# A convolution tap moved from GpSimd to ScalarE, and a weight split issued in quarters, in a two-layer hybrid sequence kernel

## The chip, the cores and the metric

The kernel runs on one core of a Trainium2 chip. The core has five engines that work side by side: TensorE (PE in the profile, with its weight loads as PEld), VectorE (DVE), ScalarE (ACT), GpSimd (POOL) and SyncE (SP), which here only issues DMAs. Each engine takes its instructions in a fixed order, and semaphores hold an instruction until what it needs is there. The metric is the device time of one execution in microseconds; smaller is better.

## What is computed

A trunk of two layers over 2048 frames of 1024 channels. Each layer normalises the residual stream, scales and shifts it with vectors that come from a conditioning input, mixes, and adds the gated result back. The first layer mixes with a linear recurrence, the second with a gated delta rule of 8 heads of 128 channels in chunks of 64 frames. Ahead of both stands a causal depthwise convolution of width 4. Cut to what matters here:

```python
def causal_dwconv(x, w):
    k = w.shape[0]
    xp = jnp.pad(x, ((0, 0), (k - 1, 0), (0, 0)))
    out = xp[:, 0:s] * w[0]
    for j in range(1, k):
        out = out + xp[:, j:j + s] * w[j]
    return out

def gated_deltanet_block(h, in_w, conv_w, a_log, dt_bias, onorm_g, out_w):
    proj = h @ in_w
    qkv = jax.nn.silu(causal_dwconv(proj[..., :o1], conv_w))
    z = proj[..., o1:o2]
    ...
    q = l2norm(q) * (GDN_DK ** -0.5)
    k = l2norm(k)
    ...
    o = chunk_gated_delta_rule(q, k, v, g, beta)
    o = o * lax.rsqrt(jnp.mean(o * o, axis=-1, keepdims=True) + EPS) * onorm_g
    return (o * jax.nn.silu(z)) @ out_w
```

All is float32. The large products are made from two parts of each operand, a rounded high part and a low part (what the rounding left): high by high, high by low and low by high.

## The kernel before

**Tiling and stages.** Channels lie on the 128 partitions, frames along the free axis in tiles of `TC` = 512. The frames go through each layer in two halves (`u` = 0 and 1, `T` = 1024 frames, two tiles each). In the second layer every half runs over heads; a head has a weight panel of 128 output channels for k, v and q each, and z panels are spread between the heads. A panel serves two jobs, one for each tile of 512 frames, and a job is 24 matmuls (8 pieces of the 1024 input channels by three products, L668) into one PSUM bank. After the second layer's heads comes the output projection with the final norm.

**Weight panels.** `panels_thread` loads a panel of 128x1024 as `raw`, ACT rounds it to the high part `whi` (L644), and in the first half GpSimd subtracts to get the low part `wlo` (L650), in one instruction of 1024 columns; `keep_thread` then writes `wlo` to HBM, and in the second half it is read back from there. `raw`, `whi` and `wlo` have two buffers each. So L650 runs 48 times: 16 panels of the first layer and 32 of the second, all in the halves u = 0.

**Convolution of the second layer.** `conv2_thread` takes a job's PSUM bank `pt`. `extend` puts it into `xe`, a tile of 4 + 512 columns: GpSimd copies the last four columns of the tile before (`carry`) or zeros into the first four (L724, L728), ACT copies the 512 out of PSUM (L730), the bank is free, and GpSimd saves the last four for the next tile (L733). Then GpSimd multiplies `xe`, shifted, by the first tap's weights into `xf` (L997), and DVE adds the other three taps with one instruction each (`taps`, L718). ACT's tanh (L1009) and a product on DVE (L1014) make the SiLU and with it `kt`, `vt` or `qt`; then `xf` is free. `xe` and `xf` have two buffers each. There are 96 such convolutions, 48 in each half. (In the first layer, `convolve` makes the last tap on ACT straight from PSUM, L746, and the others on DVE from PSUM, L756.)

**What stands around it.** From `kt` PE makes transposes and products (L1135, L1169), DVE inverts small 32x32 blocks of 8 chunks at a time in 62 short dependent steps (L1292, L1295), and then runs the recurrence over the chunks: products with the state (L1412, L1413), a combination on DVE (L1421), a product with the inverse (L1429), an ACT copy (L1435), two products (L1441, L1442) and the state's update on DVE (L1454). GpSimd has the inverse square roots (L243), masks (L1124), short copies, and part of the low parts of the activations (L572).

**The order.** The program writes the order of every engine's queue by itself. Class `Weave` runs threads against a model of time: before an instruction a thread yields the engine and an estimated cost in microseconds (`yield "pool", 2.3`), at times with the lag until its result is seen, or a set of buffers, or an event; the thread whose turn is earliest goes next, and a priority breaks ties. The engines then carry out their queues in that order, whatever the real durations are. A changed cost can so change the order of everything behind it.

## Time and profile before

| | |
|---|---|
| runs, median of 3 | 1934.21 us (1933.47 to 1941.75) |
| profiled execution, span | 1937.1 us |
| mean granted TensorE clock | 0.984 |
| first layer's input side | 0 to about 500 us |
| first layer's output projection | 500 to 668 |
| second layer, u = 0 | 668 to 1190 |
| second layer, u = 1 | 1190 to about 1743 |
| output projection, final norm | 1743 to 1937 |
| L650, 48 times | 2519 ns mean, 120.9 us |
| L997, 96 times | 782 ns mean, 75.1 us |
| L730, 96 times | 579 ns mean, 55.5 us |
| L718, 288 times | 784 ns mean, 224.9 us |
| L1014 (kt, vt, qt) | 32 times each |

The span is that of one profiled execution, from its first to its last instruction; the profile gives no time around it. The other times are whole executions. Rows of the profile name a line of the kernel, the engine, the operation and what is written from what; after "x" stands the count, then busy microseconds and the mean of one in ns, then the idle time of the engine before these instructions and what ended most of it. A chain row follows the work that ended last back from its end. A row of a line's own view gives minimum, median and maximum in ns. A row of stages has the stretch, its length, then the busy time and count for PE, PEld, DVE, ACT and POOL, the clock, the DMA share and GB/s.

### The profile page before, as it was taken

How to read it: one execution, taken by the hardware profiler on the slowest of the kernel's cores; microseconds unless marked ns; L12 is line 12 of the kernel's file. 1: busy time of each engine (PE TensorE's matmuls, PEld its weight loads, DVE VectorE, ACT ScalarE, POOL GpSimd, SP SyncE). 2: the span in 40 equal slices, each digit the busy share in tenths (PEclk: the TensorE clock that was granted, in tenths of full speed). 3: DMA queues.
4: the chain of work that ended last, by engine and by line, in shares of the span. 5: the costliest groups of instructions: out<-in, count | busy, mean ns of one | idle time of the engine just before them, and what ended most of it. 6: DMA issues, size and time to landing. Idle time of an engine off the chain costs nothing.

```text
span 1937.1 us, 31289 instructions
## 1 busy us (share of the span) xinstructions
PE 1844.0 (95%) x10286; PEld 1503.9 (78%) x10286; DVE 1471.2 (76%) x3175; ACT 1048.2 (54%) x2587; POOL 654.8 (34%) x1116
## 2 busy tenths in 40 slices
PE   6999999999899999898999999999999999999998
PEld 3787778878688877677787877788888888888887
DVE  6898998887544668869888896769777878886653
ACT  3666677667212345375565663565666656654321
POOL 3344542223100235345445543333332334411110
PEclk9999999999899999999999998999999999999999
DMA  8476746554578735446676565555365555687751
GB/s 320 116 219 189 223 138 220 175 167 138 169 204 236 208 106 145 128 111 160 166 186 141 138 158 150 149 156 158 102 163 143 140 140 139 155 246 207 230 161 66
DMA packets 511723, 322.77 MB, mean 167 GB/s; under 512 B 371268, under 2 KB 439236, under 8 KB 511560
## 3 DMA queue, kind: packets, MB, share of 16 engines
q1 hardware_dynamic: 511560, 320.77, 59.1%
q8 instruction: 81, 1.33, 0.3%
q14 instruction: 82, 0.67, 0.1%
HBM read 219.93 MB, written 100.73 MB: 166 GB/s over the span
## 4 chain that ended last, share of the span: by engine, by line
PE 61%; DVE 20%; DMA 6%; issue 4%; ACT 4%; SPq 3%; POOL 2%; DVEq 0%; POOLq 0%; ACTq 0%
PE mm L668 31%; PE mmo L668 16%; DVE xf L718 2%; DVE ttmp L1292 2%; DVE tblk L1295 2%; PE pg L807 1%; PE py L1429 1%; PE pp L1412 1%; PE pS L1442 1%; PE pqk L1257 1%; PE pS L1441 1%; PE pp L1413 1%; PE pkk L1169 1%; DVE xf L756 1%; DMA raw<-in_w 1%
## 5 line engine op out<-in xcount | busy, mean ns | idle before, releaser
L718 DVE SCALAR_TENSOR_TENSOR xf<-xe,cw_s,xf 128x512 f32<-128x512 f32 x288 | 224.9, 784 | 20.6 <-POOL xf L997 18.1
L650 POOL TENSOR_TENSOR wlo<-raw,whi 128x1024 fp32r<-128x1024 f32 x48 | 120.9, 2519 | 143.6 <-ACT whi L644 115.4
L1292 DVE TENSOR_TENSOR ttmp<-blk,tblk 128x60 f32<-128x60 f32 (+24 forms) x496 | 125.4, 253 | 16.6 <-DMA blk<-blk_d 5.4
L1295 DVE TENSOR_TENSOR tblk<-tblk,ttmp 128x60 f32<-128x60 f32 (+24 forms) x496 | 124.8, 252 | 10.7
L644 ACT CAST whi<-raw 128x1024 fp32r<-128x1024 f32 x96 | 100.2, 1044 | 50.3 <-DMA raw<-in_w 44.5
L668 PE MATMUL mmo<-oh,yh 128*128 128x512 f32 x256 | 102.1, 399 | 4.8 <-ACT oh L907 4.8
L668 PE MATMUL mm<-hh_('in2', 0)_5342,whi 128*128 128x512 f32 x256 | 105.3, 411 | 0.0
L668 PE MATMUL mm<-hh_('in2', 0)_5437,whi 128*128 128x512 f32 x256 | 105.3, 411 | 0.0
L668 PE MATMUL mmo<-ol,yh 128*128 128x512 f32 x256 | 102.2, 399 | 3.0 <-DVE ol L909 3.0
L668 PE MATMUL mm<-hh_('in2', 0)_5342,wlo 128*128 128x512 f32 x256 | 104.7, 409 | 0.0
L668 PE MATMUL mm<-hl_('in2', 0)_5343,whi 128*128 128x512 f32 x256 | 104.7, 409 | 0.0
L668 PE MATMUL mm<-hl_('in2', 0)_5438,whi 128*128 128x512 f32 x256 | 104.1, 407 | 0.0
L668 PE MATMUL mm<-hh_('in2', 1)_12030,wlo 128*128 128x512 f32 x256 | 104.1, 407 | 0.0
L668 PE MATMUL mm<-hl_('in2', 1)_12219,whi 128*128 128x512 f32 x256 | 104.0, 406 | 0.0
L668 PE MATMUL mm<-hh_('in2', 0)_5437,wlo 128*128 128x512 f32 x256 | 103.9, 406 | 0.0
L668 PE MATMUL mm<-hh_('in2', 1)_12218,whi 128*128 128x512 f32 x256 | 103.6, 405 | 0.0
L668 PE MATMUL mm<-hh_('in2', 1)_12030,whi 128*128 128x512 f32 x256 | 103.5, 404 | 0.0
L668 PE MATMUL mm<-hl_('in2', 1)_12031,whi 128*128 128x512 f32 x256 | 103.3, 403 | 0.0
L668 PE MATMUL mm<-hh_('in2', 1)_12218,wlo 128*128 128x512 f32 x256 | 103.2, 403 | 0.0
L668 PE MATMUL mmo<-ol,oh 128*128 128x512 f32 (+1 forms) x264 | 103.1, 391 | 0.0
L668 PE MATMUL mmo<-oh,ol 128*128 128x512 f32 (+1 forms) x264 | 103.1, 391 | 0.0
L668 PE MATMUL mmo<-oh,oh 128*128 128x512 f32 (+1 forms) x264 | 103.0, 390 | 0.0
(331 smaller groups left out, 5649.8 us busy)
## 6 DMA issues: line engine op xcount, KB each, us to landing
raw<-in_w SPq DMA_DIRECT2D x96, 512.0 KB, 4.2
araw<-in_ada_w SPq DMA_DIRECT2D x32, 512.0 KB, 4.3
xt<-x_d SPq DMA_DIRECT2D x32, 512.0 KB, 4.9
xt_d<-xb SPq DMA_DIRECT2D x192, 64.0 KB, 2.4
xk<-xt_d SPq DMA_DIRECT2D x24, 512.0 KB, 6.1
xt<-in_x SPq DMA_DIRECT2D x16, 512.0 KB, 4.4
ada<-in_ada_w SPq DMA_DIRECT2D x16, 512.0 KB, 8.5
y_d<-tz SPq DMA_DIRECT2D x32, 256.0 KB, 3.2
```

The source lines that it names most:

```text
L644: act.copy(hi, raw)
L650: pool.tensor_tensor(lo, raw, f(hi), ALU.subtract)
L668: pe.matmul(pt, lhsT=lhs[a][:, k, :], rhs=rhs[b][:, k, :], start=(k == 0 and n == 0), stop=(k == KT - 1 and n == 2))
L718: dve.scalar_tensor_tensor(xf, xe[:, 1 + j:1 + j + TC], wc[:, j:j + 1], xf, ALU.mult, ALU.add)
L756: dve.scalar_tensor_tensor(xf[:, 3:TC], pt[:, j:j + TC - 3], wc[:, j:j + 1], xf[:, 3:TC], ALU.mult, ALU.add)
L807: pe.matmul(pg, lhsT=a[:, g, :], rhs=b, start=(q == 0), stop=(q == 2))
L1169: pe.matmul(pkk[:, b, :], lhsT=kc, rhs=kc, start=True, stop=True)
L1257: pe.matmul(pqk[:, b, :], lhsT=kt[:, b * P:(b + 1) * P], rhs=qt[:, b * P:(b + 1) * P], start=True, stop=True)
L1292: dve.tensor_tensor(tmp, blk[:, j, j + 1:32].unsqueeze(2).to_broadcast([P, r, c_]), t[:, j, 0:c_].unsqueeze(1).to_broadcast([P, r, c_]), A ...
L1295: dve.tensor_tensor(t[:, j + 1:32, 0:c_], t[:, j + 1:32, 0:c_], tmp, ALU.subtract)
L1412: pe.matmul(pp[:, 0, :], lhsT=kc, rhs=S_, start=True, stop=True)
L1413: pe.matmul(pp[:, 1, :], lhsT=qc, rhs=S_, start=True, stop=True)
```

## The change

There are two edits and a clean-up. In the second layer's convolution the last tap (the one that lies on the frame itself) is made by ACT, straight from the PSUM bank, with the weights as a scale per partition, ahead of the copy to `xe`; GpSimd's multiply is gone, and DVE adds taps 0, 1 and 2 in place of 1, 2 and 3. For this `xf` is taken before the bank is read. In `panels_thread` the low part comes in four instructions of 256 columns each, with a planned cost of 0.63 in place of one of 2.3. The switch `POOLED`, which was empty, is dropped with what hung on it.

```diff
@@ panels_thread
-                    yield "pool", 2.3
-                    pool.tensor_tensor(lo, raw, f(hi), ALU.subtract)
+                    for q in range(0, KT, 2):
+                        yield "pool", 0.63, 0.2 if q == KT - 2 else 0.0
+                        sl = slice(q, q + 2)
+                        pool.tensor_tensor(lo[:, sl, :], raw[:, sl, :], f(hi[:, sl, :]), ALU.subtract)
                     put("raw", rtok)
                     w.spawn(keep_thread(p, lo), 5)
@@
-    def taps(xe, xf, wc, j0=1):
-        for j in range(j0, 4):
-            yield "dve", STT, 0.13 if j < 3 else 0.27
+    def taps(xe, xf, wc):
+        for j in range(3):
+            yield "dve", STT, 0.13 if j < 2 else 0.27
             dve.scalar_tensor_tensor(xf, xe[:, 1 + j:1 + j + TC], wc[:, j:j + 1], xf, ALU.mult, ALU.add)
 
-    def extend(xe, pt, mtok, bank, carry, key, g):
+    def extend(xe, xf, last, pt, mtok, bank, carry, key, g):
...
+        yield "act", 0.53, 0.0
+        act.activation(xf, pt, AF.Copy, scale=last)
         yield "act", CP
         act.copy(xe[:, 4:4 + TC], pt)
         put(bank, mtok)
@@ conv2_thread
-        yield from extend(xe, pt, mtok, bank, carry2[:, idx, :], (kind, h), u * NTC + i)
         ftok = yield slots["xf"]
-        yield "pool", 0.68
         xf = tile_([P, TC], "xf", "xf")
-        pool.tensor_scalar(xf, xe[:, 1:1 + TC], cw2_s[:, idx, 0:1], 0.0, ALU.mult, ALU.add)
+        yield from extend(xe, xf, cw2_s[:, idx, 3:4], pt, mtok, bank, carry2[:, idx, :], (kind, h), u * NTC + i)
         ttok = yield slots["tt"]
-        if kind in POOLED:
...
-        yield from taps(xe, xf, cw2_s[:, idx, :], 2 if kind in POOLED else 1)
+        yield from taps(xe, xf, cw2_s[:, idx, :])
```

## The prediction

> **What bounds the kernel now.** I read the page first, then the chain of waits by stage, then the groups of instructions and the waits of the two halves of the second layer (u = 0 from 668 us to 1190, u = 1 from there to 1743), and last two short pieces of the timeline.

> ```profile
> PE 1844.0 (95%) x10286; PEld 1503.9 (78%) x10286; DVE 1471.2 (76%) x3175; ACT 1048.2 (54%) x2587; POOL 654.8 (34%) x1116
> PE 61%; DVE 20%; DMA 6%; issue 4%; ACT 4%; SPq 3%; POOL 2%; DVEq 0%; POOLq 0%; ACTq 0%
> ```

> PE carries 61% of the chain that ended last, DVE 20%; GpSimd, which the change relieves, only 2%. The stages differ, though. These are the chain by line, 668 to 1190 and then 1190 to 1743, and the busy time by engine of the same two stages.

> ```profile
> by line: PE mm L668 27.3%; DVE xf L718 7.6%; DVE ttmp L1292 7.4%; DVE tblk L1295 6.3%; issue 4.9%; PE pqk L1257 2.0%; PE pab L1055 1.4%; ACT junkq L1208 1.3%; PE pkk L1169 1.3%; PE px L1363 1.3%; DVE kt L1014 1.2%; DMA pq<-q_d 1.2%; SPq L13
> ```
> ```profile
> by line: PE mm L668 54.7%; PE pp L1412 2.7%; PE py L1429 2.6%; PE pS L1442 2.4%; DMA zs<-z_d 2.4%; PE pkk L1169 2.4%; PE pp L1413 2.3%; PE pS L1441 2.3%; PE pqk L1257 1.9%; PE pr L1373 1.7%; issue 1.4%; DMA vn<-v_d 1.3%; PE px L1334 1.3%; D
> ```
> ```profile
> 668.00:1190.00 522.00, 484.68 (x3068) 398.07 (x3067) 420.68 (x1036) 293.67 (x895) 245.38 (x436) 0.98 0.57 145
> 1190.00:1743.00 553.00, 546.62 (x3600) 455.21 (x3599) 432.02 (x1222) 337.69 (x1039) 183.47 (x414) 0.99 0.57 152
> ```

> In the first half DVE's taps (L718), its two lines of the small inverses (L1292, L1295) and the product L1014 hold at least 22.5% of the chain, the projection's matmuls 27.3%: DVE and PE share the bound. In the second half the matmuls of L668 alone have 54.7%, and no DVE line is above 1.3%. A microsecond won for DVE is worth something in the first half and next to nothing in the second.

> What makes the first half so? The taps and the inverse there, then the same groups in the second half:

> ```profile
> L718 DVE SCALAR_TENSOR_TENSOR xf<-xe,cw_s,xf 128x512 f32<-128x512 f32 x144 | 116.3, 811 | 13.5 <-POOL xf L997 12.1
> L1292 DVE TENSOR_TENSOR ttmp<-blk,tblk 128x54 f32<-128x54 f32 (+24 forms) x224 | 65.3, 292 | 7.0 <-DMA tt_d<-ttmp 1.5 <-DMA blk<-blk_d 1.4
> L1295 DVE TENSOR_TENSOR tblk<-tblk,ttmp 128x54 f32<-128x54 f32 (+24 forms) x224 | 60.7, 271 | 4.8
> L650 POOL TENSOR_TENSOR wlo<-raw,whi 128x1024 fp32r<-128x1024 f32 x30 | 74.9, 2496 | 81.7 <-ACT whi L644 64.3 <-DMA wlo_d2z<-wlo 8.5 <-DMA q_d<-tb 4.2
> L997 POOL TENSOR_SCALAR xf<-xe,cw_s 128x512 f32<-128x512 f32 x48 | 37.7, 785 | 1.7 <-DMA raw<-in_w 1.5
> ```
> ```profile
> L718 DVE SCALAR_TENSOR_TENSOR xf<-xe,cw_s,xf 128x512 f32<-128x512 f32 x144 | 108.6, 757 | 7.1 <-POOL xf L997 6.0
> L1295 DVE TENSOR_TENSOR tblk<-tblk,ttmp 128x60 f32<-128x60 f32 (+24 forms) x248 | 59.0, 238 | 5.3
> L1292 DVE TENSOR_TENSOR ttmp<-blk,tblk 128x60 f32<-128x60 f32 (+24 forms) x248 | 55.0, 222 | 9.2 <-DMA blk<-blk_d 4.1
> ```

> L650 runs only in the first half, L997 equally in both (48 each). Without L650 a tap costs 757 ns, with it 811; the inverse's lines 222 and 238 against 292 and 271. The differences come to 54 ns x 144 + 70 ns x 224 + 33 ns x 224 = 31 us of DVE time beside 74.9 us of L650, 0.41 us for each. How, the timeline shows:

> ```profile
> 746.18 2.48 POOL L650 TENSOR_TENSOR wlo<-raw,whi 128x1024 fp32r<-128x1024 f32 x1 [2.79 <-ACT whi L644]
> 746.18 0.21 DVE L1292 TENSOR_TENSOR ttmp<-blk,tblk 128x52 f32<-128x52 f32 x1
> 746.42 2.30 DVE L1295 TENSOR_TENSOR tblk<-tblk,ttmp 128x52 f32<-128x52 f32 x1
> ...
> 758.78 2.39 POOL L650 TENSOR_TENSOR wlo<-raw,whi 128x1024 fp32r<-128x1024 f32 x1
> 758.86 2.86 DVE L1161 TENSOR_TENSOR ec<-ec,cc 128x512 f32<-128x512 f32 x1
> 761.11 0.66 POOL L733 COPY carry<-xe 128x4 f32<-128x4 f32 x1
> 761.75 0.69 POOL L997 TENSOR_SCALAR xf<-xe,cw_s 128x512 f32<-128x512 f32 x1
> 761.89 0.63 DVE L1295 TENSOR_TENSOR tblk<-tblk,ttmp 128x65 f32<-128x65 f32 x1
> ```

> A DVE instruction of 0.21 us takes 2.30 and ends just behind L650. Then they alternate: L1161 ends at 761.72, the carry copy waits for it (0.66 us), L997 goes, and the next step of the inverse takes 0.63. Only one of the two moves at a time.

> **The change part by part.** The prices come from these rows (all taps of the trace; ACT's PSUM copy and the carry; a copy with an immediate scale and one with a scale per partition, both 128x128 from PSUM; ACT's tap in the first layer, with scale and bias; GpSimd's subtract of a quarter's size):

> ```profile
> L718 DVE SCALAR_TENSOR_TENSOR xf<-xe,cw_s,xf x288: 702/748/2885, 676.8 to 1698.3; 128x512 f32<-128x512 f32 x144
> L730 ACT COPY xe<-mm x96: 561/582/594, 675.0 to 1691.3; 128x512 f32<-128x512 f32 x96
> L733 POOL COPY carry<-xe x96: 178/188/749, 675.8 to 1691.9; 128x4 f32<-128x4 f32 x96
> L1435 ACT ACTIVATE yt<-py x128: 253/278/291, 817.6 to 1802.9; 128x128 f32<-128x128 f32 x128
> L1468 ACT ACTIVATE t<-pp,eg x120: 346/368/373, 820.8 to 1801.8; 128x128 f32<-128x128 f32 x120
> L746 ACT ACTIVATE xf<-mm,cb_s,cw_s x32: 762/778/782, 56.3 to 473.4; 128x509 f32<-128x509 f32 x32
> L875 POOL TENSOR_TENSOR gl<-gw,gh x16: 732/1053/1502, 53.0 to 468.7; 128x256 fp32r<-128x256 f32 x16
> ```

> *ACT's new tap.* A per-partition scale adds 368 - 278 = 90 ns, so 582 + 90 = 0.67 us, between 0.58 (the copy) and 0.78 (L746). 48 a half are +32 us of ACT in each, 294 to 326 of 522 and 338 to 370 of 553. Behind it wait the xe copy, the release of the PSUM bank (0.67 us later: PE has a second bank, and with 30 panels of two jobs in 522 us a job comes every 8.7; uncovered it would be 32 us a half), then the tanh, the key's scalings, the recurrence's yt. An ACT instruction finds a tap running one time in 16 (32/522) and waits 0.34 us: 895 x 0.06 x 0.34 = 18 us of delay spread over all of them, and ACT lines hold little of the chain: +1.5 us a half (0 to 9).

> *L997 goes.* From the job's end to the first tap stood copy, carry and L997: 0.58 + 0.28 + 0.78 = 1.64 us; now tap and copy, 1.25, with no place in GpSimd's queue. DVE makes three taps either way. DVE's waits for L997 in the first half (us, times, longest):

> ```profile
> DVE xf L718 <- POOL xf L997: 12.1, 7, 4.1
> ```

> At least 0.39/1.64 of it goes (3 us), at most all; I take 8, since 1.7 us a time, and 4.1 once, is more than L997 lasts: the rest was GpSimd's queue, L650 in it. What is late next is DVE's own queue. Second: the 37.7 us in which L997 kept DVE out. At L650's rate this is 37.7 x 0.41 = 15 us; from below, the second half, where L997 runs just as much and a tap is 757 ns against an overall median of 748, the inverse's two lines 222 and 238: (9 x 144 + 16 x 248) ns = 5 us for all of GpSimd. I take 6, nearer to that, since it holds L997 itself. 14 us of DVE time at a worth between 0.225 (the chain share) and 1; in the middle, 0.6: -8.5 us (bounds: 8 us at 0.225, -2, to 27 us at 1, -27). In the second half 6.0 us of waits at a worth of 0.2 at most: -1.

> *Four pieces.* A piece is L875's form: 0.73 us alone, so 2.93 a panel for L650's 2.40; beside a busy DVE 1.05, 4.2 a panel. That is +16 to +54 us for GpSimd over 30 panels, against 37.7 that L997 gives back: no relief of its queue, 0 on the chain. For DVE: if every piece found a gap, its 31 us would go; if each hold costs as before, 2.93/2.40 makes it 38. From -31 to +7 then; I take 0, as at 761 us the two took turns, and a DVE with work queued loses one hold at each turn. In the first layer (16 panels) a low part comes up to 1.8 us later; two panels' buffers cover it, and PE waited for wlo just twice in the whole trace (the view of waits: us, times, longest):

> ```profile
> PEld mm L668 <- POOL wlo L650: 2.5, 1, 2.5
> PE mm L668 <- POOL wlo L650: 2.1, 1, 2.1
> ```

> Without that cover it would be 16 x 1.8 = 29 us. I take 0. No DMA is added; wlo's store to HBM leaves after the last piece.

> *Sum:* first half -8.5 + 1.5, second half -1 + 1, first layer 0: **-7 us**. The profiled execution spans 1937.1 us, which would be 1930; the page shows no time around the span, and it lies 2.9 above the median of the runs, 1934.2, so I forecast **1927 us**. Its own range, 1918 to 1936, lets DVE's worth and the pieces go half way to their bounds.

> The planner writes all orders anew from its changed costs (0.53 on ACT for 0.68 on GpSimd, four times 0.63 for 2.3, with room for other GpSimd work between), so every queue shifts a little, in the first layer too; no row prices that, and I leave it to the range.

> **The rivals.** *Larger gain, 1914:* DVE gets back every microsecond that L997 held, as the step of 2.30 us lost its whole time beside L650. Then 37.7 us and all 12.1 us of the wait go, the pieces' longer holds add 30 x (2.93 - 2.40) = 16, and 34 us at 0.6 make -20. For it: the rows at 746 us. Against it: 0.41 us lost for each held one, and the cheap second half. It decides where DVE always has an instruction of that kind in front.

> [...]

> *Nothing, 1933:* the taps were late because of DVE, not L997. DVE is busy 421 of 522 us, and its 12.1 us of waits are small beside the rest; -1 remains.

> *Slower, 1946:* ACT's tap needs a free xf buffer (two, each held until L1014), and now it is ACT that waits for it, in front of everything else in its queue; before, GpSimd did.

> ```profile
> 749.60 0.57 ACT L730 COPY xe<-mm 128x512 f32<-128x512 f32 x1
> 760.51 0.56 ACT L730 COPY xe<-mm 128x512 f32<-128x512 f32 x1
> 762.44 0.71 DVE L1014 SCALAR_TENSOR_TENSOR vt<-tt,xf 128x512 f32<-128x512 f32 x1
> ```

> The convolution evacuated at 749.60 gave its xf back at 763.15; the copy two convolutions later began at 760.51, so a tap in its place would have stopped ACT for 2.6 us. L730 and L1014 pair off in order, 96 each:

> ```profile
> L1014 DVE SCALAR_TENSOR_TENSOR kt<-tt,xf x32: 662/685/2872, 680.9 to 1665.1; 128x512 f32<-128x512 f32 x32
> L1014 DVE SCALAR_TENSOR_TENSOR vt<-tt,xf x32: 673/686/2110, 690.4 to 1683.8; 128x512 f32<-128x512 f32 x32
> L1014 DVE SCALAR_TENSOR_TENSOR qt<-tt,xf x32: 641/689/2095, 723.0 to 1700.7; 128x512 f32<-128x512 f32 x32
> ```

> Compared row by row, 8 of 94 pairs overlap so, 11 us in all. If the new order, whose planned convolutions are shorter than DVE's real ones, doubles this, ACT stands 22 us, and at 0.6, with nothing gained, that is +13 less 1, about +12. It decides from about 16 such stops on.

> **How the numbers follow.** A measurement of this kernel tells about 0.5% from no change, 9.7 us: below 1924.5 is faster, above 1943.9 slower. Forecast 0.48 (0.19 of it below 1924.5), larger gain 0.24, nothing 0.11, slower 0.17 (0.01 of it within). Faster 0.19 + 0.24 = 0.43; same 0.29 + 0.11 + 0.01 = 0.41; slower 0.16. The range, 1908 to 1944, takes in the larger gain and the slower rival's near half.

> **What would show it.** Right: L718's wait for its releaser in the first half falls from 12.1 to about 4 and its mean from 811 ns by some 20; the inverse's 292 and 271 hardly move, because the pieces take turns; the new ACT line has 96 x 0.67 us; PE's idle before pk and pqk falls. Larger gain: taps under 780 ns and the inverse under 260 in the first half. Nothing: the waits before L718 go, and others before DVE grow by as much. Slower: ACT's new line waits for L1014 many times, and PE behind yt. I am wrong if the stage that changes is not 668 to 1190.

## The result, and the profile after

The changed kernel is **slower**: a median of 1950.7 us in 5 runs (1946.5 to 1953.9) beside 1934.2 for before, ratio 1.0072 with a 95% interval of [1.0058, 1.0086]. A second comparison on another chip gave 1.0057 [1.0038, 1.0077]. The forecast was 1927, the range 1908 to 1944, and the chance given to slower by over 0.5% was 0.16. The profiled execution spans 1946.3 us (before: 1937.1).

The page of the changed kernel, busy time by engine and the chain by engine:

```profile
PE 1844.6 (95%) x10286; PEld 1507.8 (77%) x10286; DVE 1440.2 (74%) x3175; ACT 1101.9 (57%) x2683; POOL 617.8 (32%) x1164
PE 58%; DVE 16%; DMA 9%; ACT 6%; issue 4%; SPq 4%; POOL 3%; DVEq 0%; POOLq 0%; ACTq 0%
```

DVE has 31 us less to do (1471.2 to 1440.2) and falls from 20% of the chain to 16%; ACT has 54 more, GpSimd 37 less. All of that is what the change meant, and the time is longer. In the chain DMA went from 6% to 9% and ACT from 4% to 6%.

Where the time goes is best seen by PE's busy time in the same stretches. Columns: stretch in us, length, then busy time and count of PE, PEld, DVE, ACT and POOL, granted clock, DMA share, GB/s. Before:

```profile
668.00:940.00 272.00, 250.96 (x1483) 204.13 (x1481) 210.51 (x493) 140.41 (x407) 123.64 (x212) 0.97 0.52 136
940.00:1120.00 180.00, 169.86 (x1164) 141.12 (x1163) 152.98 (x389) 113.56 (x361) 91.29 (x171) 0.99 0.63 152
1120.00:1240.00 120.00, 110.52 (x687) 89.95 (x686) 96.17 (x268) 66.96 (x198) 48.15 (x74) 0.96 0.59 159
...
1690.00:1760.00 70.00, 69.21 (x470) 57.64 (x469) 55.34 (x143) 38.40 (x100) 11.37 (x26) 1.00 0.83 244
```

The changed kernel:

```profile
668.00:940.00 272.00, 260.54 (x1532) 212.35 (x1531) 207.41 (x501) 161.15 (x443) 121.12 (x246) 0.99 0.55 144
940.00:1120.00 180.00, 164.82 (x1146) 137.91 (x1147) 141.27 (x386) 118.57 (x370) 78.73 (x173) 0.95 0.60 144
1120.00:1240.00 120.00, 107.41 (x732) 87.63 (x731) 92.67 (x271) 71.24 (x209) 41.37 (x77) 0.94 0.58 158
...
1690.00:1760.00 70.00, 63.91 (x492) 52.80 (x491) 50.44 (x140) 35.44 (x93) 6.77 (x16) 0.95 0.73 209
```

PE gains 9.6 us of work by 940, loses 5.0 by 1120 and 3.1 by 1240, and 5.3 more at the seam to the output projection. The granted clock is lower in these three stretches too. So the gain is there by 940, and it is given back later. To follow this through the kernels that come below I use one reading of my own: the matmuls of a trace in order of time, weighted by their size, and how much later than in before each amount of work is done (us; negative is ahead; columns are times of before; each row is one profiled execution, and that of e6 was 7 us below its median). The columns 475, 668, 1700 and end hardly depend on how a matmul is weighted; those between move by several microseconds with it (at 1000, the changed kernel has -7 to -17 by other weights), so they tell places and not sizes.

| kernel | 475 | 668 | 1000 | 1120 | 1220 | 1260 | 1700 | 1745 | end |
|---|---|---|---|---|---|---|---|---|---|
| changed | 4.7 | 3.3 | -11.0 | -1.3 | 4.6 | 2.5 | -0.6 | 8.7 | 9.2 |
| order of before, both works (e6) | -3.1 | -3.1 | -14.0 | -17.0 | -23.2 | -23.8 | -25.2 | -23.1 | -23.1 |
| new order, old work (e7) | 8.1 | 3.4 | 5.0 | 17.5 | 27.6 | 25.5 | 28.1 | 34.6 | 35.6 |
| planned cost 2.31 for 2.30 (e8) | 1.9 | 4.0 | -8.8 | -9.5 | -12.1 | 2.9 | 4.8 | 4.7 | 4.7 |
| planned cost 2.29 for 2.30 (e12) | 3.6 | 4.4 | 12.4 | 9.9 | 1.7 | 11.6 | 12.6 | 13.5 | 18.7 |

### The profile page after: what moved, and what is told of

Read it like the earlier page. It is cut to its first block, busy times and chain, and to the rows that moved or that the text cites. A ratio compares the mean times of both kernels' runs of the same rounds, so it can differ in the third digit from the quotient of the medians.

```text
span 1946.3 us, 31418 instructions
## 1 busy us (share of the span) xinstructions
PE 1844.6 (95%) x10286; PEld 1507.8 (77%) x10286; DVE 1440.2 (74%) x3175; ACT 1101.9 (57%) x2683; POOL 617.8 (32%) x1164
## 4 chain that ended last, share of the span: by engine, by line
PE 58%; DVE 16%; DMA 9%; ACT 6%; issue 4%; SPq 4%; POOL 3%; DVEq 0%; POOLq 0%; ACTq 0%
PE mm L669 29%; PE mmo L669 15%; DVE xf L719 2%; DVE tblk L1290 2%; DVE ttmp L1287 2%; DMA oraw<-in_ow 2%; PE py L1424 1%; PE pS L1436 1%; PE pS L1437 1%; PE pkk L1164 1%; POOL wlo L651 1%; PE pp L1407 1%; PE pp L1408 1%; DMA araw<-in_ada_w 1%; PE pg L810 1%
## 5 line engine op out<-in xcount | busy, mean ns | idle before, releaser
L719 DVE SCALAR_TENSOR_TENSOR xf<-xe,cw_s,xf 128x512 f32<-128x512 f32 x288 | 221.0, 770 | 15.9 <-ACT xe L733 10.6
L651 POOL TENSOR_TENSOR wlo<-raw,whi 128x256 fp32r<-128x256 f32 x192 | 160.8, 868 | 150.7 <-ACT whi L643 117.6
L643 ACT CAST whi<-raw 128x1024 fp32r<-128x1024 f32 x96 | 100.1, 1043 | 60.7 <-DMA raw<-in_w 52.2
L1290 DVE TENSOR_TENSOR tblk<-tblk,ttmp 128x60 f32<-128x60 f32 (+24 forms) x496 | 119.5, 241 | 10.6 <-POOL tblk L1281 0.3
L669 PE MATMUL mm<-hh_('in2', 0)_5491,whi 128*128 128x512 f32 x256 | 105.0, 410 | 1.5 <-DVE tf L1362 1.5
L669 PE MATMUL mm<-hh_('in2', 0)_5396,whi 128*128 128x512 f32 x256 | 105.0, 410 | 1.5 <-DVE tz L1020 0.9
L669 PE MATMUL mm<-hl_('in2', 1)_12214,whi 128*128 128x512 f32 x256 | 105.6, 413 | 0.0
L669 PE MATMUL mm<-hl_('in2', 0)_5492,whi 128*128 128x512 f32 x256 | 104.4, 408 | 0.0
L669 PE MATMUL mm<-hh_('in2', 1)_12213,whi 128*128 128x512 f32 x256 | 104.3, 407 | 0.1
L669 PE MATMUL mm<-hl_('in2', 0)_5397,whi 128*128 128x512 f32 x256 | 104.3, 408 | 0.0
L669 PE MATMUL mm<-hh_('in2', 0)_5491,wlo 128*128 128x512 f32 x256 | 104.3, 408 | 0.0
L669 PE MATMUL mm<-hh_('in2', 0)_5396,wlo 128*128 128x512 f32 x256 | 104.0, 406 | 0.0
L669 PE MATMUL mm<-hh_('in2', 1)_12213,wlo 128*128 128x512 f32 x256 | 103.8, 405 | 0.0
```

The source lines that it names most:

```text
L643: act.copy(hi, raw)
L651: pool.tensor_tensor(lo[:, sl, :], raw[:, sl, :], f(hi[:, sl, :]), ALU.subtract)
L669: pe.matmul(pt, lhsT=lhs[a][:, k, :], rhs=rhs[b][:, k, :], start=(k == 0 and n == 0), stop=(k == KT - 1 and n == 2))
L719: dve.scalar_tensor_tensor(xf, xe[:, 1 + j:1 + j + TC], wc[:, j:j + 1], xf, ALU.mult, ALU.add)
L1290: dve.tensor_tensor(t[:, j + 1:32, 0:c_], t[:, j + 1:32, 0:c_], tmp, ALU.subtract)
```

## The experiments

The theories when the runs began: **A**, the work of the change gains, and the order that the planner made anew from the changed costs loses more; **B**, ACT's tap costs, by its wait for xf or by holding the bank; **C**, the pieces cost, through GpSimd's longer sum. The runs were made on five chips, each beside before on the same chip, with medians of before from 1936.4 to 1938.5; a ratio is always to before on its own chip.

**One edit alone, as planned.** e1 is the changed kernel with the low part in one instruction again, e2 is before with the four pieces.

e1, against the changed kernel:

```diff
-                    for q in range(0, KT, 2):
-                        yield "pool", 0.63, 0.2 if q == KT - 2 else 0.0
-                        sl = slice(q, q + 2)
-                        pool.tensor_tensor(lo[:, sl, :], raw[:, sl, :], f(hi[:, sl, :]), ALU.subtract)
+                    yield "pool", 2.3
+                    pool.tensor_tensor(lo, raw, f(hi), ALU.subtract)
```

e2, against before: the same lines the other way round.

> The ACT tap alone, the low part of a panel in one instruction as before. Theory A (the work itself gained some 12 us in the first half of the second layer, and the new order lost it and more at two places, about 1040 to 1080 and 1700 to 1780): the first layer as before to 1 us, the middle of the first half 5 to 12 us ahead of before by matmuls done, and the end anywhere between 1920 and 1950, depending on where the output weights' loads fall. Theory B (ACT's tap costs: its queue stands before the tap for xf, and 54 us more of ACT): 1945 or more, with ACT's waits on L1009 or the new line. Theory C (the four pieces cost, through GpSimd's 160.8 us for 120.9): 1934 or less, since they are not there.

> The four pieces alone, the first tap on GpSimd as before. Theory A: the first layer loses about 3 us as in the changed kernel, DVE is held up less by L650 in the first half, the end between 1920 and 1950. Theory B: about 1934, since ACT has nothing new. Theory C: 1945 to 1950, the whole loss.

Measured: e1 1967.5 us, 1.0156 [1.0121, 1.0190]; e2 1949.1, 1.0066 [1.0047, 1.0084]. Each edit alone is slower, the tap alone slower than both together: as costs of work these do not add. Taken by themselves the two runs do not decide for A: e1 lies above A's 1950 and in B's range, and in its first half ACT's tap stood 7.7 us for `xf`, a sign that B named; e2 fits A and C. But each also has an order of its own, so what follows must hold the order. No run has e1's order with the work of before, so how its 1.6% divides stays open.

**The work without the order, the order without the work.** e3 and e5 leave every planned cost as in before, so that each engine's queue is as before but for the exchanged instructions. e3 issues the four pieces in one planned step. e5 lets ACT make the last tap in L997's place, read from `xe`, so that the bank and `xf` are taken as in before; DVE adds the other three. e6 is both. e4 keeps the work of before and tells the planner of four steps; e7 has the whole order of the changed kernel and the work of before.

e3, e5 and e4, each against before:

```diff
                     yield "pool", 2.3
-                    pool.tensor_tensor(lo, raw, f(hi), ALU.subtract)
+                    for q in range(0, KT, 2):
+                        sl = slice(q, q + 2)
+                        pool.tensor_tensor(lo[:, sl, :], raw[:, sl, :], f(hi[:, sl, :]), ALU.subtract)
```
```diff
         yield "pool", 0.68
         xf = tile_([P, TC], "xf", "xf")
-        pool.tensor_scalar(xf, xe[:, 1:1 + TC], cw2_s[:, idx, 0:1], 0.0, ALU.mult, ALU.add)
+        act.activation(xf, xe[:, 4:4 + TC], AF.Copy, scale=cw2_s[:, idx, 3:4])
...
-            dve.scalar_tensor_tensor(xf, xe[:, 1 + j:1 + j + TC], wc[:, j:j + 1], xf, ALU.mult, ALU.add)
+            dve.scalar_tensor_tensor(xf, xe[:, j:j + TC], wc[:, j - 1:j], xf, ALU.mult, ALU.add)
```
```diff
-                    yield "pool", 2.3
+                    for q in range(0, KT, 2):
+                        yield "pool", 0.63, 0.2 if q == KT - 2 else 0.0
                     pool.tensor_tensor(lo, raw, f(hi), ALU.subtract)
```

e7, against the changed kernel (with the low part as in e4):

```diff
         yield "act", 0.53, 0.0
-        act.activation(xf, pt, AF.Copy, scale=last)
...
+        pool.tensor_scalar(xf, xe[:, 1:1 + TC], cw2_s[:, idx, 0:1], 0.0, ALU.mult, ALU.add)
         ttok = yield slots["tt"]
...
-            dve.scalar_tensor_tensor(xf, xe[:, 1 + j:1 + j + TC], wc[:, j:j + 1], xf, ALU.mult, ALU.add)
+            dve.scalar_tensor_tensor(xf, xe[:, 2 + j:2 + j + TC], wc[:, j + 1:j + 2], xf, ALU.mult, ALU.add)
```

> The low part in four instructions, but back to back within the one planned step of 2.3, so that every other instruction keeps its order of before. What is left is the effect of the pieces themselves. Theory A: within 5 us of 1934, rather below, as in the changed kernel DVE was lengthened beside these instructions by some 14 us less. Theory C: 1940 or more, as GpSimd is busy 30 to 40 us longer.

> The planner is told of four steps of 0.63, but one instruction is issued after the last, so that only the order changes and the costs of a few steps in the plan. Theory A: it moves the time by several us in one direction or the other, 5 to 15 from 1934, though no instruction is added or removed. Theories B and C: 1934 within 3.

> ACT makes the last tap in place of GpSimd's first, in the place that GpSimd's step had in the plan, so that no other instruction changes its order. It reads xe and not the PSUM bank, so that the bank and xf are taken as before. Theory A (work gains, order loses): 0.2 to 0.8% faster than before (4 to 15 us). Theory B (ACT's tap costs): slower by 0.5% or more, with yt, kd or tt late behind it on ACT.

> That tap and the four pieces in one planned step, all in the order of before. Theory A: faster than the pieces in the old order alone (ratio 0.9924), about 0.985 to 0.992. Theory B: between the two parts, 0.993 or more.

> The plan of the changed kernel, so its order of all other instructions, with the work of before in it: GpSimd's first tap and one instruction for the low part after the fourth planned piece. Theory A: slower than the changed kernel by what the work gains, so 1.012 to 1.02 of before. Theory B: faster than the changed kernel (1.0072), as ACT has its time back.

| work | order of before | order of the changed kernel |
|---|---|---|
| of before | 1 | 1.0198 [1.0164, 1.0232] (e7) |
| pieces | 0.9924 [0.9901, 0.9948] (e3) | 1.0143 [1.0119, 1.0167] (e13) |
| ACT's tap | 0.9988 [0.9969, 1.0007] (e5) | |
| both | 0.9921 [0.9898, 0.9945] (e6) | 1.0072 [1.0058, 1.0086] |

e4 gave 1.0150 [1.0112, 1.0188]. It has the plan of e2, so these two are one more order: the pieces gain 0.8% in that one too. So the work gains in either order, 0.8% in the old one and 1.3% in the new; the order costs 2.0% with the old work and 1.5% with the new. A holds; B and C fall as reasons for the changed kernel's loss. In microseconds of 1937: -15 of work in the old order, +29 of order, together the +14 measured. Sizes were missed on the way: A expected at most 5 us from e3, which gained 15, at most 15 from e4, which lost 28, and 0.2 to 0.8% from e5, which gained nothing that can be told.

The 2.0% holds more than the order. In e7 and e13 GpSimd's tap stands in a place that was planned for ACT, and DVE waits longer for it: in the second half 20.9 us in e13 for 6.0 in before (us, times, longest):

```profile
DVE xf L719 <- POOL xf L998: 20.9, 18, 3.1
```

The same instructions in both orders are e6 above (0.9921) and e14 below (1.0043), both with the tap read from `xe`: between them the order costs 1.2%, 24 us.

Where the new order loses with no new work in it shows in the same three stretches of the first half (e7):

```profile
668.00:940.00 272.00, 252.66 (x1448) 205.49 (x1446) 210.49 (x479) 142.79 (x409) 124.44 (x218) 0.99 0.52 137
940.00:1120.00 180.00, 159.28 (x1053) 131.76 (x1054) 145.99 (x387) 103.64 (x334) 76.33 (x143) 0.92 0.58 141
1120.00:1240.00 120.00, 106.12 (x715) 85.94 (x714) 94.55 (x259) 61.28 (x191) 46.69 (x84) 0.91 0.60 153
```

It is level up to 940 and then 10.6 and 4.4 us of PE's time behind before. The changed kernel's losses lie in the same stretches: its new work makes them smaller, and does not cause them. Within these stretches the new order has one place that the old one lacks. The changed kernel there:

```profile
1040.00:1050.00 10.00, 5.96 (x36) 4.55 (x34) 6.08 (x11) 2.85 (x6) 5.44 (x11) 1.00 0.29 49
1050.00:1060.00 10.00, 6.06 (x95) 5.53 (x96) 5.47 (x19) 3.66 (x10) 0.82 (x3) 0.52 0.76 196
```

PE is busy 12.0 of 20 us, waits for `qt` and for the operands of the inverse's small products, and has its clock at half for 17.1 us from 1050.5. All seven profiles with this order (the changed kernel twice, e7, e11, e13, e14, e17) have 13.7 to 20.5 us of half clock there; before, e3, e5 and e6 have no such stretch over 6.8 us between 700 and 1180. Which step of the order opens this place was not tried.

**Is it this order, or any new one?** e8 changes one planned cost by 10 ns and nothing else; in e12 it is 2.29.

```diff
-                    yield "pool", 2.3
+                    yield "pool", 2.31
```

> Before with the planned cost of the low part at 2.31 in place of 2.30 and nothing else: no instruction is added, removed or lengthened, but the queues come out in another order. Theory A: it moves the time by a visible amount, 0.3% or more in either direction, which would be the size of the lottery that any changed cost draws from. Theory B: within 0.2%.

> The kernel of before with the planned cost of the low part at 2.29 in place of 2.30, all work as before. The order stays the same in the first layer and differs from about 680 us on. If any re-planned order costs something, as with 2.31 (1.0044 [1.0028, 1.006]), this one has a ratio of 1.003 to 1.02 with the loss behind 680 us and none before. If 2.31 was an accident and small changes of the order cancel, it is 0.998 to 1.002.

e8: 1945.1 us, 1.0044 [1.0028, 1.0060]. e12: 1957.8, 1.0118 [1.0084, 1.0152]. With e4 and e7 these are four other orders of exactly the old work: 1.0044, 1.0118, 1.0150 and 1.0198. Their losses lie at different places (the table: e8 is 12 us ahead at 1220 and loses 15 by 1260). So the order of before is a good one among those that the same planner gives for nearly the same costs, and a re-plan is a draw of 0.4 to 2% to the worse, as far as four draws tell (in e4 and e7 part of the work stands in places planned for other work; e8 and e12 are free of that, at 0.4 and 1.2%).

**One place of the loss, undone.** e11 is the changed kernel with the loads of the final norm at a lower priority. Up to about 1640 us its order is the changed kernel's.

```diff
-        w.spawn(o_loads_thread(), 3)
+        w.spawn(o_loads_thread(), 5)
```

> The changed kernel with the loads of the final norm (on, zs) planned at a lower priority. The order is that of the changed kernel up to about 1620 us and another one behind it, the work is the same. If the 9 us that the changed kernel loses between 1700 and 1745 us come from its order at that place, where DVE stands for zs in front of the z panel's product, most of them come back: ratio 0.9955 to 1.002, and by equal TensorE work the kernel stands level with before at 1700 and within 4 us of it at the end. If they come from the new work (ACT's tap, the pieces), which this leaves alone, the ratio stays at 1.005 to 1.009 and the loss of 7 to 10 us shows at the same place.

1944.5 us, 1.0035 [1.0018, 1.0053]: about half of the loss is gone (40% by the second comparison); the ratio is a little above the range that was expected if this place was the cause. By equal work it stood at 1.5 us at 1700 and 5.0 at the end, so it lost 3.5 where the changed kernel lost 9.8 (7.8 in its second profile). What happened there, on DVE and then on PE in the changed kernel (start, us, instruction; in brackets what it waited for):

```profile
1707.24 0.22 DVE L1290 TENSOR_TENSOR tblk<-tblk,ttmp 128x54 f32<-128x54 f32 x1
1710.13 1.22 DVE L1560 TENSOR_TENSOR zs<-on,zs 128x1024 f32<-128x1024 f32 x1 [2.67 <-DMA zs<-z_d]
...
1714.47 0.68 DVE L1020 SCALAR_TENSOR_TENSOR tz<-tz,mm 128x512 f32<-128x512 f32 x1
```
```profile
1706.89 1.16 PE L1252 MATMUL pqk<-qt,kt 128*128 128x128 f32 x8 [2.23 <-DVE qt L1009]
...
1712.70 0.39 PE L669 MATMUL mm<-hh_('in2', 1)_12213,whi 128*128 128x512 f32 x1
1715.21 1.25 PE L1368 MATMUL pr<-ac,tf 64*64 64x64 f32 x16 [2.12 <-DVE tz L1020]
1716.39 0.79 PE L669 MATMUL mm<-hl_('in2', 1)_12214,whi 128*128 128x512 f32 x1
```

The order puts `zs` (L1560) into DVE's queue ahead of the z panel's product (L1020). The load of `zs` is late, DVE stands 2.67 us, eleven other instructions follow, and PE waits 2.12 us for L1020, after 2.23 for `qt`. In ten-microsecond stretches from 1700, changed kernel and then e11:

```profile
1700.00:1710.00 10.00, 7.78 (x93) 6.24 (x92) 5.38 (x18) 4.34 (x10) 0.00 (x0) 1.00 1.00 224
1710.00:1720.00 10.00, 7.80 (x40) 6.06 (x39) 8.89 (x30) 3.89 (x15) 1.47 (x3) 0.80 0.94 291
1720.00:1730.00 10.00, 10.00 (x50) 8.60 (x49) 6.99 (x35) 4.25 (x16) 0.00 (x0) 0.85 0.16 49
```
```profile
1700.00:1710.00 10.00, 10.00 (x101) 7.61 (x99) 5.73 (x19) 3.77 (x10) 0.00 (x0) 1.00 1.04 290
1710.00:1720.00 10.00, 9.70 (x62) 8.35 (x62) 9.14 (x34) 4.33 (x18) 1.44 (x3) 1.00 0.97 263
1720.00:1730.00 10.00, 10.00 (x57) 8.64 (x56) 9.09 (x34) 6.88 (x21) 2.61 (x3) 1.00 0.35 99
```

The changed kernel loses 4.4 us of PE's time to stops in the first two stretches and has a mean granted clock of 0.80 and 0.85 in the last two; e11 has 0.3 us of stops and a clock of 1.00.

**The tap, in the new order.** e13 is the changed kernel with GpSimd's tap as in e7, its pieces kept. e14 exchanges ACT's two instructions on a job, so that the bank is free after the first. e17 is e14 with e11's late loads, e18 the changed kernel once more beside it.

e14, against the changed kernel:

```diff
         yield "act", 0.53, 0.0
-        act.activation(xf, pt, AF.Copy, scale=last)
+        act.copy(xe[:, 4:4 + TC], pt)
         yield "act", CP
-        act.copy(xe[:, 4:4 + TC], pt)
+        act.activation(xf, xe[:, 4:4 + TC], AF.Copy, scale=last)
```

> The order of the changed kernel with its four pieces, but GpSimd's first tap as before (ACT's slot for the tap stays empty, GpSimd's multiply follows the carry copy in its queue). With the old work this order gave 1.0198, with both new works 1.0072. If the tap is worth as little in the new order as in the old one (0.9988 there) and the pieces are the whole gain, this is 1.005 to 1.010, that of the changed kernel. If the tap is worth something in an order that was planned for it, as I forecast, it is 1.012 to 1.017. If ACT's tap from PSUM costs, the kernel is faster than the changed one: 0.999 to 1.004.

> The changed kernel with ACT's two instructions on a job exchanged: the copy to xe first, then the tap, read from xe in place of PSUM. The bank comes free one instruction (0.67 us) sooner, and a full xf can no longer hold the bank; the carry copy too can go 0.67 us sooner. All orders stay. If the tap in front of the bank's release costs, the ratio falls to 0.999 to 1.005; if it is covered, as the prediction had it, 1.005 to 1.009 as for the changed kernel.

> The changed kernel with both single edits that made it faster: the final norm's loads at a lower priority (1.0035 alone) and ACT's tap behind the copy, from xe (1.0043 alone). If each is real, their differences from the changed kernel, 0.0037 and 0.0029, add: 0.999 to 1.002. If the tap's place in front of the bank's release cost nothing and 1.0043 was the spread between chips, the ratio is that of the late loads alone: 1.003 to 1.005.

> The changed kernel itself, beside the one above on one chip, to carry their difference. By its first comparison 1.0058 to 1.0086; a lower ratio here would say that the two single differences of 0.0037 and 0.0029 were partly its own spread.

e13: 1964.4 us, 1.0143 [1.0119, 1.0167], so in the new order exchanging the tap is worth 0.7% (14 us). As DVE's waits above show, that is the price of GpSimd's tap in a place not planned for it as much as the worth of ACT's; these runs do not part the two. e14: 1945.6, 1.0043 [1.0028, 1.0059]; e17: 1942.6, 1.0021 [1.0005, 1.0037]; e18: 1947.8, 1.0057 [1.0038, 1.0077]. Read from `xe` behind the copy, the tap is 0.0029 below the first comparison of the changed kernel and 0.0014 below the second, and it takes the same 0.0014 off the late loads' 1.0035, all within the intervals. e14 fell into the range that was expected for a cost, e17 between its two. Whether the tap costs anything ahead of the bank's release stays open; by these medians it is 0.1 to 0.3%.

**Why the pieces gain.** In the order of before, e9 cuts the low part in two and e10 in eight; e15 takes quarters in the first layer and eighths in the second, e16 adds the tap of e5. e15 is shown; `step` is 4 throughout in e9 and 1 in e10.

```diff
                     yield "pool", 2.3
-                    pool.tensor_tensor(lo, raw, f(hi), ALU.subtract)
+                    step = 2 if name[0] == "in1" else 1
+                    for q in range(0, KT, step):
+                        sl = slice(q, q + step)
+                        pool.tensor_tensor(lo[:, sl, :], raw[:, sl, :], f(hi[:, sl, :]), ALU.subtract)
```

> The kernel of before with the low part in two instructions of 512 columns inside the one planned step of 2.3, so that nothing else moves; it stands between one instruction (1.0) and four (0.9924 [0.9901, 0.9948]). If a DVE instruction caught beside a low-part instruction stands still for what is left of it, the mean time caught falls with the length of the instruction: from about 1.8 us a hit with one to 0.46 with four, and halves should have most of the gain: ratio 0.993 to 0.997, 5 to 13 us, and DVE taps of the first half near 811 ns, the inverse's steps between 266 and 292. If only pieces short enough to fit into DVE's own gaps help, halves have nearly none of it: 0.998 to 1.001.

> The same with eight instructions of 128 columns in the one planned step. If the length of a hold is what costs DVE, eighths gain once more, but little, as each also pays GpSimd's fixed cost: 0.989 to 0.993, and the wlo group of the first half may go from 95.1 us to 110 or more. If the sum of the holds counts (the view of the prediction, which took the pieces as 0), eighths lose against quarters, since the sum grows: 0.996 to 1.004.

> The kernel of before with the low part in four instructions in the first layer and in eight in the second, all inside the one planned step of 2.3. By equal TensorE work eighths lost 11 us up to 668 and won 21 from there to 1220, quarters -1 and 15. If the first layer's loss of the eighths is the sum of GpSimd's holds (84 us there in place of 46) and the second layer's gain is their length, the two parts add: -1 and -21, less what eighths gave back behind 1220 (some 5 us), 16 to 22 us in all, ratio 0.9885 to 0.992. If the profile of eighths was one lucky execution in its second layer, this is 0.9925 to 0.996.

> The same with ACT's tap (from xe) in place of GpSimd's, order unchanged. Beside quarters that tap added nothing that could be told (0.9921 for 0.9924). If the convolution's place off GpSimd only counts where GpSimd is loaded, it may count beside eighths, where DVE's waits for GpSimd's tap rose from 12.1 to 18.3 us: 0.985 to 0.989. If not: equal to the kernel with quarters and eighths alone within 0.0015.

| instructions a panel | ratio | GpSimd's sum on it, us | time that DVE loses beside it, us (times) |
|---|---|---|---|
| 1 (before) | 1 | 120.9 | 63.6 (35) |
| 2 (e9) | 0.9948 [0.9925, 0.9970] | 134.8 | 55.3 (62) |
| 4 (e3) | 0.9924 [0.9901, 0.9948] | 159.5 | 47.2 (102) |
| 8 (e10) | 0.9962 [0.9943, 0.9981] | 201.3 | 28.4 (138) |
| 4, then 8 (e15) | 0.9916 [0.9885, 0.9946] | 186.7 | 33.1 (130) |
| 4, then 8, ACT's tap (e16) | 0.9870 [0.9838, 0.9901] | 189.1 | 37.1 (140) |

The last column is my own reading, good to a few microseconds: how much longer than the lower quartile of its group a DVE instruction took, where it lay beside a low part, in both layers. GpSimd's sum rises, and DVE loses less. The place that the prediction showed at 746 us, in e3 with the same order:

```profile
745.86 0.21 DVE L1294 TENSOR_TENSOR ttmp<-blk,tblk 128x52 f32<-128x52 f32 x1
745.88 2.89 POOL L652 TENSOR_TENSOR wlo<-raw,whi 128x256 fp32r<-128x256 f32 x4 [2.81 <-ACT whi L644]
746.11 0.64 DVE L1297 TENSOR_TENSOR tblk<-tblk,ttmp 128x52 f32<-128x52 f32 x1
746.78 0.66 DVE L1294 TENSOR_TENSOR ttmp<-blk,tblk 128x50 f32<-128x50 f32 x1
747.47 0.67 DVE L1297 TENSOR_TENSOR tblk<-tblk,ttmp 128x50 f32<-128x50 f32 x1
```

They take turns, as forecast. But beside one long instruction DVE ended one step (2.30 us); beside the four pieces it ended three (0.64, 0.66, 0.67) in 2.0 us. The groups of the first half, 668 to 1190, in e3 and in e10:

```profile
L720 DVE SCALAR_TENSOR_TENSOR xf<-xe,cw_s,xf 128x512 f32<-128x512 f32 x144 | 116.3, 811 | 14.9 <-POOL xf L999 13.5
L1294 DVE TENSOR_TENSOR ttmp<-blk,tblk 128x60 f32<-128x60 f32 (+24 forms) x240 | 64.5, 269 | 6.7 <-DMA tt_d<-ttmp 1.4 <-POOL tblk L1288 0.9
L1297 DVE TENSOR_TENSOR tblk<-tblk,ttmp 128x60 f32<-128x60 f32 (+24 forms) x240 | 63.9, 266 | 5.3 <-POOL tblk L1288 0.2
...
L652 POOL TENSOR_TENSOR wlo<-raw,whi 128x256 fp32r<-128x256 f32 x120 | 95.1, 823 | 79.7 <-ACT whi L644 60.6 <-DMA wlo_d2z<-wlo 7.9 <-DMA q_d<-tb 4.7
```
```profile
L720 DVE SCALAR_TENSOR_TENSOR xf<-xe,cw_s,xf 128x512 f32<-128x512 f32 x144 | 114.1, 795 | 19.7 <-POOL xf L999 18.3
L1297 DVE TENSOR_TENSOR tblk<-tblk,ttmp 128x60 f32<-128x60 f32 (+24 forms) x234 | 59.7, 255 | 5.2
L1294 DVE TENSOR_TENSOR ttmp<-blk,tblk 128x60 f32<-128x60 f32 (+24 forms) x234 | 59.2, 253 | 6.9 <-DMA blk<-blk_d 2.0 <-DMA ac<-tt_d 0.6
...
L652 POOL TENSOR_TENSOR wlo<-raw,whi 128x128 fp32r<-128x128 f32 x240 | 117.1, 524 | 80.7 <-ACT whi L644 56.5 <-DMA wlo_d2z<-wlo 8.3 <-DMA q_d<-tb 4.5
```

The inverse's short steps profit: 292 and 271 ns in before, 269 and 266 with quarters, 253 and 255 with eighths; the taps, as long as a quarter, hardly (811, 811, 795). The total of e10 fits the other view at first sight: it was expected at 0.989 to 0.993 if the length of a hold counts and from 0.996 if their sum does. By equal work it divides: eighths alone lose 11 us by 668 in the first layer and gain 21 from there to 1220 (quarters lose nothing and gain 15). With quarters in the first layer e15 stood at 0.9 at 668 and at -18.8 at 1220, so the first layer's loss is that of its eighths; by what wait was not shown (PE waited 0.8 us for `wlo` there). e16 is the **fastest**: 1910.8 us, better than both kernels; whether its tap adds to e15 is not settled, as the intervals overlap.

## Why the prediction was wrong, point by point

- **The step that failed: the re-planned order.** The prediction saw that every queue is written anew, found "no row prices that", and left it to the range, at nothing. With the old work that order costs 2.0% (38 us), with the same instructions in both orders 1.2% (24 us): three to five times the change that was forecast. The sum was made for work inserted into a fixed order. In that frame it was too small (7 us for the 15 of e6), and its parts were exchanged: the tap, from which all of its gain was to come, gave nothing that can be told, and the pieces, taken as 0, gave all of it.
- **Four pieces taken as 0**: the term has a wrong size. The bounds were -31 to +7 us of DVE's time for the 30 panels of the first half; the runs show -16 (63.6 to 47.2) for all 48, some two thirds of it on these 30, and 0.76% of the time in the old order (15 us), 0.55% in the new. That "the two took turns" was read rightly, as the rows at 746 us show in before and in e3; the mistake is in "loses one hold at each turn", taken for a loss of the same sum, since a hold is then a third as long (823 ns for 2496) and a step that is caught loses 0.45 us for 2.1 (0.66 and 2.30 in those rows, less 0.21). The bound of +7 let the loss grow with the sum of the holds; in e3 that sum rose from 74.9 to 95.1 us in the first half, and the time fell.
- **L997 goes, -8.5 us.** In the old order nothing that can be told (0.9988), though DVE's steps became shorter there too. The wait ahead of the first tap stayed and only changed its name, from 12.1 us for GpSimd to 14.1 for ACT:

```profile
L718 DVE SCALAR_TENSOR_TENSOR xf<-xe,cw_s,xf 128x512 f32<-128x512 f32 x144 | 115.0, 802 | 15.4 <-ACT xf L997 14.1
L1292 DVE TENSOR_TENSOR ttmp<-blk,tblk 128x54 f32<-128x54 f32 (+24 forms) x223 | 63.8, 286 | 8.5 <-DMA tt_d<-ttmp 1.5 <-DMA blk<-blk_d 1.4 <-DMA vn<-v_d 1.0
L1295 DVE TENSOR_TENSOR tblk<-tblk,ttmp 128x54 f32<-128x54 f32 (+24 forms) x222 | 55.4, 249 | 4.8
```

  In the new order, where ACT's tap has the place that was planned for it and GpSimd's has not, the exchange is worth 14 us. The forecast lies between; the worth of one edit depends on the order around it, which the prediction did not consider.
- **ACT's tap, 0.67 us**: right in its length (its +1.5 us a half entered the sum as 1.5 and 1, which changes nothing). DVE's and ACT's groups of the changed kernel, 668 to 1190:

```profile
L719 DVE SCALAR_TENSOR_TENSOR xf<-xe,cw_s,xf 128x512 f32<-128x512 f32 x144 | 113.7, 792 | 9.0 <-ACT xe L733 4.9 <-POOL nk L1149 1.7 <-POOL xe L725 1.3
L1290 DVE TENSOR_TENSOR tblk<-tblk,ttmp 128x60 f32<-128x60 f32 (+24 forms) x235 | 63.1, 268 | 5.1 <-POOL tblk L1281 0.3
L1287 DVE TENSOR_TENSOR ttmp<-blk,tblk 128x60 f32<-128x60 f32 (+24 forms) x236 | 59.0, 250 | 14.1 <-DMA blk<-blk_d 3.4 <-DMA tt_d<-ttmp 2.8 <-DMA v_d<-tb 2.2
```
```profile
L731 ACT ACTIVATE xf<-mm,cw_s 128x512 f32<-128x512 f32 x48 | 32.8, 683 | 18.9 <-PE mm L669 14.3 <-DVE qt L1009 2.8 <-DVE vt L1009 1.6
```

  A tap costs ACT 683 ns. The other signs: the taps' mean fell by 19 ns (20 forecast), their waits from 12.1 us only to 4.9 for ACT and some 3 for GpSimd (4 forecast), and the inverse's first line fell by 42 ns, where it was to stay: 23 ns of that came with the pieces alone in the old order, and 24 with the new order and the old work (268 ns in e7), so it is not the pieces' alone. PE's idle before pk fell, from 10.6 us to 4.8; before pqk it did not, 7.3 and 7.7.
- **The slower rival, 1946**: nearly the time, by coincidence, and not the cause. ACT's tap waits for xf 2.8 + 1.6 us in the first half, where the rival needed 22, and e14, where the tap no longer stands ahead of the bank's release, is 0.1 to 0.3% faster by its median.
- **"Wrong if the stage that changes is not 668 to 1190"**: the gain is there (9.6 us of PE's time by 940) and so is most of the loss, but the first layer lost 3 us (in e7 with the old work as well, so by the order) and the stretch from 1700 on nearly ten, and neither was in the sum.

## What to carry to other kernels

Where a planner writes the order, a changed cost buys a new order, and here that alone moved the time by 0.4 to 2%, in three of four draws more than either edit did with the order held: judge an edit with the order held, and only then look for an order for it. A long GpSimd instruction beside chains of short DVE steps was worth cutting, though its sum grew: quarters gained (0.9924, with 159.5 us for 120.9), eighths gained more in the second layer (21 us for 15) and lost in the first (11 us), so how far to cut has to be measured. And the price of a wait in one order is not its price in another: the exchange of the tap was worth nothing that can be told in the old one and 14 us in the new.

## What the runs showed of the hardware that was not expected

**A stop of PE cost more than its length here.** After the stop of 2.12 us that ended at 1715.21 the matmul's record went from 0.39 us to 0.79. The trace's record of the granted clock has it at one half from 1716.1 for 6.8 us, which the rows of ten microseconds show as 0.80 and 0.85; in before, whose PE was busy 9.72 of 10 us there, it stayed at 1.00. Before, 1710 to 1730:

```profile
1710.00:1720.00 10.00, 9.72 (x58) 7.92 (x57) 7.86 (x29) 2.28 (x6) 0.23 (x1) 1.00 0.73 233
1720.00:1730.00 10.00, 10.00 (x57) 8.65 (x56) 9.37 (x30) 7.95 (x21) 1.54 (x3) 1.00 0.57 169
```

In the 3.4 us ahead of the fall in the changed kernel PE was busy 1.28. These 3.4 us are the step of the record itself: in the traces of before and of the changed kernel all 19 stretches of half clock between the first 60 us and the last 20 are 3.41 us long or two, three or five times that.

```profile
1230.00:1240.00 10.00, 4.92 (x86) 3.65 (x87) 4.82 (x16) 3.57 (x9) 2.63 (x4) 0.60 0.77 219
1240.00:1250.00 10.00, 10.00 (x57) 6.25 (x56) 5.67 (x9) 5.24 (x11) 2.87 (x3) 0.72 0.00 1
```

So part of what an order loses is the slower clock behind its stops. In all, the clock is at half for 62 us in before, 42 in e6, 75 in the changed kernel and 95 in e7. A matmul's record then takes twice as long (0.79 for 0.39 us), so each of these microseconds costs at most half of one, and the 32 more of e7 are at most 16 of the 36 us by which its profile is longer: an estimate from these figures. A place where PE only just keeps busy was worth more than its idle microseconds in this kernel: the changed kernel stood 4.4 us from 1700 to 1720, and the 6.8 us of half clock are at most 3.4 more.
